# Output projection of a hybrid decoder layer: seven block products in place of eight, activations of projection and feed-forward in paired tiles, the second norm split in wide pieces

## The chip, the cores and the metric

The kernel runs on one core of a Trainium2 chip. The metric is the device time of one execution in microseconds (us). A core has a matrix engine (TensorE, PE in the profile, with its weight loads as PEld), a vector engine (VectorE, DVE), a scalar engine (ScalarE, ACT), a general engine (GpSimd, POOL) and a queue engine that issues transfers (SyncE, SP). Each works through its own list of instructions in order; they wait for each other through semaphores.

## The reference: one decoder layer

512 positions, width 1024, everything in float32. What matters here:

```python
h = rmsnorm(x, norm1_w)
proj = h @ w_in                       # q, k, v of 6 + 6 attention heads, and GLA's inputs
y_a = dilated_attention(...)          # 6 heads of 64
y_b = gla(...)                        # 4 heads of 64, gated linear attention
y_c = moba_attention(...)             # 6 heads of 64
mix = concat([y_a, y_b, y_c])         # 512 x 1024
x = x + mix @ w_out                   # the output projection, 1024 x 1024
h2 = rmsnorm(x, norm2_w)
x = x + square(relu(h2 @ w_ff1)) @ w_ff2     # 1024 -> 4096 -> 1024
out = rmsnorm(x, final_norm_w)
```

## The kernel before

**Products in three parts.** TensorE multiplies in fp32r, a shorter format than float32. So every operand is split in two: a high part, cast on ScalarE (`wh` of a weight, `mh`, `yh`, `Ah` of an activation), and the low rest, a subtraction on VectorE (`wl`, `ml`, `yl`, `Al`). A product is then three matmuls: high by high, high by low, low by high. A weight piece is 128x1024; it comes by a DMA on SP's queue into a raw tile (`wraw`, `w2raw`), and its split takes one cast and one subtraction.

**The stages.** `main` (line 1364) is the list of TensorE's dense work: the first projection of GLA's inputs (`av`, `bq`, `bk` in the profile), the values and gates (`vps`), q and k of six pairs of heads (`qkps`), the values of the second group (`vps`), the output projection `out_proj` (line 1009, `ops`), and the feed-forward network `ffn` (line 1277). Attention is filled in between: scores (`sps`), transposes of the softmax (`ptp`), and the product with the values (`po`) in `values` (line 784), once for each two pairs of heads. GLA ends with two transposes (`yp`). Each result for the mix goes through `mix_out` (line 514), which makes `mh` and `ml` straight from PSUM, for one of eight blocks of 128 columns of the mix.

**The output projection** makes four tiles of 128 positions (t) by two halves of 512 columns. Each tile and half is a sum over the 8 blocks of the mix, three matmuls of 128x512 each. It begins with the blocks that are there first (the order is in `KO`), for t = 0 and 1, and does the last two blocks, from the last heads, after `po` of these heads. When a tile's half is done, `x2_out` (line 981) adds it to the residual `x3` (VectorE) and takes the sum of squares (ScalarE, `junk`); after the second half `inv_rms` (line 969) makes the factor `y` in four tiny steps that go between ScalarE and VectorE. `y_out` (line 991) scales the tile (`y0`, shown as `y`), turns it with eight transposes of 128x128 (`yps`), and splits the result in pieces of 128x128, with the norm's weight: 4 casts and 4 subtractions for each half.

**The feed-forward network** goes in four quarters of 1024 hidden columns. `f` is the first product; ScalarE applies relu into a tile `h` of 128x512 and a square follows. The second product is done in blocks by a scheme of Strassen's kind: `h` of a quarter and the quarter of `w_ff2` are each cut into 2x2 blocks, `a_parts` (line 1072) makes sums and differences of the activation blocks (`s`), `sums2` (line 340) those of the weight blocks, and seven products of blocks (`products`, line 372; `f2X` to `f2W`) replace eight. The results are added to `x3` by `add` (line 1150). A block of the activations is two tiles of 128x2x256; since `h` is 128x512 with both halves of the positions in one row, `a_parts` reads a block in pieces of 128x256. The first four columns of `f` are made in two halves of 256 positions, since only the first tiles are normalised by then.

**What sets the order.** Every stage is a generator that gives out instructions; `Plan` (line 98) takes the instruction that could start first by its own table of costs (ties by priority), and the list of each engine is written in that order. Nothing is reordered on the chip. Buffers are tokens: 23 large ones of 128x1024 (`big`), pairs of split weights (`w`), pairs of split activations (`part`), and the PSUM banks. All instructions are recorded at line 128 of the file, so in the profile they are told apart by their tiles.

Of the kernel before, what the change touches and what calls it, by code (L numbers as in the profile page):

```python
# [30 lines left out]
NH = 4  # L31


class Op:


    def __init__(self, eng, method, args, kw):
# [9 lines left out]
        self.outs = [o.tensor.name for o in outs]  # L47
        self.ins = [a.tensor.name for a in inner]
# [148 lines left out]
def hybrid_block_kernel(ctx: ExitStack, tc: tile.TileContext, x0_d, xT_d, x_d, w0_d, wv_d, wqk_d, wo_d, w1_d, w2_d,  # L197
                        ba_d, wa2_d, gw_d, fw_d, rb_d, oh_d, cst_d, lm_d, out_d):
# [15 lines left out]
    def big(name, dt=F32, shape=(128, 1024)):  # L214
        return wp.tile(list(shape), dt, name=name, tag="big", bufs=BIGS)

# [34 lines left out]
    nwh = consts.tile([128, KT], F32)  # L251
# [11 lines left out]
    xh = [slot("xh", F32R) for _ in range(KT)]  # L263
    xl = [slot("xl", F32R) for _ in range(KT)]
# [10 lines left out]
    def fetch():  # L275
        for key, src, n in pieces[1:]:
# [36 lines left out]
    def cut():  # L313
        for key, src, n in pieces:
# [6 lines left out]
            if key[0] == "1" and (key[1] % 8 == 0 and key[1] or key[1] == 31):  # L321
                yield from cut2((key[1] - 1) // 8)
# [5 lines left out]
    def fetch2():  # L328
        yield ("wait", ("raw", ("1", 5)))
        for c in range(NC):  # L330
# [7 lines left out]
            spawn(sums2(c), 4)  # L338

# [32 lines left out]
    def products(c):  # L372


        if c < NC - 1:
# [5 lines left out]
    def cut2(c):  # L381
        for o, (n, *_) in enumerate(products(c)):
# [9 lines left out]
            for _ in range(2):  # L392
                if n > 2:
                    give("big")
                    give("raw2")
# [55 lines left out]
    def row_scale():  # L451
# [16 lines left out]
        yield DVE.tensor_scalar(nwh, nw[:, 1], -0.5, None, op0=OP.mult)  # L468
# [43 lines left out]
    mh, ml = [None] * 8, [None] * 8  # L512
# [38 lines left out]
    def gla():  # L551
# [117 lines left out]
        yield ("wait", "G")  # L669
        for i in range(2):  # L670
# [9 lines left out]
            yield DVE.tensor_tensor(oB[i], oB[i], G[i], op=OP.mult)  # L680
        for f in range(2):
            r = "gm"[f] * (1 + f)
# [4 lines left out]
            spawn(mix_out(3 + f, yp, r), 1)  # L687
# [48 lines left out]
    def attention(e):  # L736
# [3 lines left out]
        for p in range(6):  # L740
# [14 lines left out]
            if ("sps", p) in plan.done:  # L755
# [3 lines left out]
                if p == 4:  # L759
                    give("w")  # L760
                    give("w")
                if p == 5:
                    for _ in range(3):
                        give("big")
                    give("w")
                    fire("scores")
# [17 lines left out]
    def values():  # L784


        for ps_ in ((0, 1), (2, 3), (4, 5)):
# [24 lines left out]
            for p, po, r in zip(ps_, pos, "og"):  # L812
                spawn(mix_out(p if p < 3 else p + 2, po, r), 1)
# [29 lines left out]
    def v_out(g, t, acc):  # L843
# [12 lines left out]
        yield DVE.tensor_scalar(sg, rg, 80.0, None, op0=OP.min)  # L856
        yield DVE.tensor_tensor(rg, rg, gw, op=OP.mult)
# [80 lines left out]
    def gate(i):  # L938


        sg, rg = gates[i]
# [4 lines left out]
        yield DVE.scalar_tensor_tensor(d, sg, 1.0, y, op0=OP.add, op1=OP.mult)  # L946
        yield DVE.scalar_tensor_tensor(d, d, -2.0, y, op0=OP.add, op1=OP.mult)
        yield DVE.tensor_tensor(rg, d, rg, op=OP.mult)
# [6 lines left out]
    yh, yl = [slot("yh", F32R) for _ in range(KT)], [slot("yl", F32R) for _ in range(KT)]  # L955
# [25 lines left out]
    def x2_out(t, half, acc, r):  # L981
        yield DVE.tensor_tensor(x3[t, half], acc, x3[t, half], op=OP.add)
        give(r)
        yield from square_sum(t, half)
        if half:
# [4 lines left out]

    def y_out(t, half, y):
        y0 = slot("y0")
        yield Any(DVE.tensor_scalar(y0, x3[t, half], y, None, op0=OP.mult), ACT.activation(y0, x3[t, half], AF.Copy, scale=y))
        r = ("pt", "pt") if t != 1 else ("o", "g")
        r = r[half]
# [3 lines left out]
        ts = slice(t * 128, (t + 1) * 128)  # L999
        ks = range(half * 4, half * 4 + 4)  # L1000
        src = [pt[:, i * 128:(i + 1) * 128] for i in range(4)]
        for i, k in enumerate(ks):
            yield ACT.activation(yh[k][:, ts], src[i], AF.Copy, scale=nwh[:, k:k + 1])
        for i, k in enumerate(ks):
            yield DVE.scalar_tensor_tensor(yl[k][:, ts], src[i], nwh[:, k:k + 1], f32(yh[k][:, ts]), op0=OP.mult, op1=OP.subtract)
            fire(("y", t, k))
        give(r)

    def out_proj():

        w = {}
        accs = {}

        def step(t, i, halves=(0, 1)):
            k = KO[i]
            if i not in w:
                yield ("wait", ("w", ("o", i)))
                w[i] = loaded.pop(("o", i))
            yield ("wait", ("mix", k))
            wh, wl = w[i]  # L1020
            ts = slice(t * 128, (t + 1) * 128)
            for half in halves:
                fs = slice(half * 512, half * 512 + 512)
                yield [PE.matmul(accs[t][half], xx[k][:, ts], ww[:, fs], start=(i + j == 0), stop=(i == 7 and j == 2))
                       for j, (xx, ww) in enumerate(((mh, wh), (ml, wh), (mh, wl)))]

        def take(t):
            r = "mm" if t % 2 == 0 else "s"
            accs[t] = []
# [499 lines left out]
```

## Time and profile before

| | |
|---|---|
| median of 3 runs | 585.29 us (585.05 to 585.51) |
| the profiled execution | 586.21 us, span from first to last instruction 584.4 us |
| TensorE busy | 575.6 us, 98% of the span |
| VectorE busy | 420.8 us, 72% |
| ScalarE busy | 325.4 us, 56% |
| DMA | 62.00 MB, mean 106 GB/s |
| granted TensorE clock, mean | 0.997 |

Busy time is the time in which an engine has an instruction in work. TensorE's instructions overlap (the next begins before the one before has left the array), so the mean duration of a matmul is longer than the step from one to the next, and the step is read from a row of the chain: its time over its count. The chain of waits, followed back from the last instruction, tells which engine sets the time at each moment. In the order listings below, as in the profile, `out<-in` names the tiles, and `x4` is a row that stands four times.

### The profile page before, as it was taken

The numbers are of one execution on the slowest core, as the hardware profiler recorded it, in microseconds if no ns is written. First come the engines' busy times: TensorE is split into PE (matmuls) and PEld (weight loads), VectorE is DVE, ScalarE is ACT, GpSimd is POOL, SyncE is SP. The second block draws the span as 40 slices with busy tenths as digits, with TensorE's granted clock in tenths as the row PEclk, the third lists the DMA queues.
The fourth block names the chain that finished last, engine by engine and source line by source line (L and its number), as shares of the span: only waits on it lengthen the run. The fifth ranks groups of instructions, "written<-read, shape, count | busy, mean of one in ns | idle before, by whom it ended". The sixth has DMA issues, their size and how long they took to land.

```text
span 584.4 us, 8148 instructions
## 1 busy us (share of the span) xinstructions
PE 575.6 (98%) x3030; PEld 478.9 (82%) x3030; DVE 420.8 (72%) x812; ACT 325.4 (56%) x611; POOL 19.0 (3%) x36
## 2 busy tenths in 40 slices
PE   9999999999999999999999999999999999999995
PEld 8988888977888588899888888888888888888884
DVE  6879999987774405566479954599925699755896
ACT  6756476887787305546457334575244664354654
POOL 7000000000000000000000000000000000000021
PEclk9999999999999999999999999999999999999998
DMA  9920334322342600194004732025621046201003
GB/s 313 341 74 2 109 89 147 91 73 85 119 123 73 252 1 0 59 372 127 20 1 153 243 109 72 1 72 183 213 73 37 1 138 223 72 1 36 1 0 146
DMA packets 20696, 62.00 MB, mean 106 GB/s; under 512 B 2482, under 2 KB 3168, under 8 KB 20656
## 3 DMA queue, kind: packets, MB, share of 16 engines
q1 hardware_dynamic: 19728, 59.84, 31.3%
q0 software_dynamic: 640, 1.10, 0.6%
q8 instruction: 24, 0.39, 0.3%
q10 hardware_dynamic: 288, 0.53, 0.3%
q14 instruction: 16, 0.13, 0.1%
HBM read 59.34 MB, written 2.13 MB: 105 GB/s over the span
## 4 chain that ended last, share of the span: by engine, by line
PE 97%; DVE 1%; ACT 0%; issue 0%; DVEq 0%
PE f L128 30%; PE f2X L128 14%; PE qkps L128 11%; PE vps L128 8%; PE ops L128 7%; PE f2Z L128 6%; PE f2Y L128 4%; PE sps L128 3%; PE po L128 2%; PE ptp L128 2%; PE av L128 2%; PE f2W L128 2%; PE lp L128 1%; PE bk L128 1%; PE bq L128 1%; PE op L128 1%
## 5 line engine op out<-in xcount | busy, mean ns | idle before, releaser
L128 DVE TENSOR_TENSOR wl<-wraw,wh 128x1024 fp32r<-128x1024 f32 (+1 forms) x68 | 78.3, 1160 | 39.6 <-ACT wh L128 33.9
L128 PE MATMUL f<-yh,wh 128*128 128x512 f32 (+1 forms) x288 | 105.3, 366 | 0.0
L128 PE MATMUL f<-yl,wh 128*128 128x512 f32 (+1 forms) x288 | 105.3, 365 | 0.0
L128 PE MATMUL f<-yh,wl 128*128 128x512 f32 (+1 forms) x288 | 105.2, 365 | 0.0
L128 ACT ACTIVATE wh<-wraw 128x1024 fp32r<-128x1024 f32 (+1 forms) x67 | 67.2, 1013 | 58.4 <-PE f L128 23.2
L128 DVE TENSOR_TENSOR wl<-w2raw,wh 128x1024 fp32r<-128x1024 f32 x48 | 59.4, 1243 | 48.5 <-ACT wh L128 44.7
L128 ACT ACTIVATE wh<-w2raw 128x1024 fp32r<-128x1024 f32 x48 | 50.3, 1054 | 49.2 <-PE f L128 39.7
L128 PEld LDWEIGHTS f<-yl,wh 128*128 128x128 f32 x288 | 54.3, 189 | 8.8
L128 PEld LDWEIGHTS f<-yh,wh 128*128 128x128 f32 x288 | 54.3, 189 | 8.7
L128 PEld LDWEIGHTS f<-yh,wl 128*128 128x128 f32 x288 | 54.3, 189 | 8.7
L128 PE MATMUL f2X<-wl,Ah 128*128 128x512 f32 (+1 forms) x128 | 49.4, 386 | 0.0
L128 PE MATMUL f2X<-wh,Al 128*128 128x512 f32 (+1 forms) x128 | 49.4, 386 | 0.0
L128 PE MATMUL f2X<-wh,Ah 128*128 128x512 f32 (+1 forms) x128 | 49.4, 386 | 0.0
L128 PE MATMUL qkps<-xh,wh 128*128 128x512 f32 x96 | 39.3, 409 | 1.0 <-DVE tk L128 1.0
L128 PE MATMUL qkps<-xh,wl 128*128 128x512 f32 x96 | 37.6, 391 | 0.0
L128 PE MATMUL qkps<-xl,wh 128*128 128x512 f32 x96 | 37.5, 390 | 0.0
L128 ACT ACTIVATE P<-P,mn 128x512 f32<-128x512 f32 (+3 forms) x48 | 26.5, 553 | 14.1 <-DVE mn L128 14.0
L128 ACT ACTIVATE h<-f 128x512 f32<-128x512 f32 x32 | 18.6, 582 | 18.7 <-PE f L128 18.7
L128 DVE CUSTOM_DVE_ANT_0 P<-sps,nb 128x512 f32<-128x512 f32 (+3 forms) x48 | 22.4, 483 | 8.5 <-PE sps L128 7.9
L128 ACT ACTIVATE junk<-x 128x512 f32<-128x512 f32 (+1 forms) x16 | 9.8, 615 | 32.8 <-DVE x L128 32.8
L128 PEld LDWEIGHTS f2X<-wh,Al 128*128 128x128 f32 x128 | 24.1, 188 | 4.9
L128 PEld LDWEIGHTS f2X<-wh,Ah 128*128 128x128 f32 x128 | 24.0, 188 | 4.9
(248 smaller groups left out, 1187.8 us busy)
## 6 DMA issues: line engine op xcount, KB each, us to landing
wraw<-in_w SPq DMA_DIRECT2D x32, 512.0 KB, 3.6
w2raw<-in_w SPq DMA_DIRECT2D x32, 512.0 KB, 4.3
wraw<-in_wqk SPq DMA_DIRECT2D x12, 512.0 KB, 4.0
wraw<-in_wv SPq DMA_DIRECT2D x8, 512.0 KB, 6.4
wraw<-in_wo SPq DMA_DIRECT2D x8, 512.0 KB, 3.6
nb<-tab SPq DMA_DIRECT2D x12, 256.0 KB, 4.0
x<-in_x SPq DMA_DIRECT2D x8, 256.0 KB, 4.8
wraw<-in_w SPq DMA_DIRECT2D x7, 264.0 KB, 5.2
```

What stands on the lines that cost most here:

```text
L128: getattr(getattr(self.nc, op.eng), op.method)(*op.args, **op.kw)
```

## The change

The output projection becomes chunk 0 of the same block scheme that the second product of the feed-forward network uses, which has chunks 1 to 4 now. `w_out` is handed in with its rows in the order of `KO` and joined to `w_ff2`. The mix is written to PSUM-sized halves of large tiles (`halves`, `mix_out`), as plain float32, so that `a_parts(0)` can form and split block sums; `fetch0` loads `w_out` in eight pieces (`woraw`), `sums0` makes the block sums of the weights, `cut2(0)` splits them, and `ff2(0)` runs the seven products in the order 0, 4, 6, 2, 3, 1, 5. `products` gives for each the accumulator (X, W or Y) and the block (half of the positions, half of the columns) to which it adds. The positions' second half (t = 2, 3) is complete first, so the first columns of `f` begin with it.

`h` is now a tile of 128x2x2x256, shared by two columns of `f`, in which the two tiles of one block lie together; `a_parts` works on 128x512 where it worked on 128x256. `y_out` multiplies by the norm's weight before the transposes (a row of weights, `nw2`, broadcast to 128 partitions, is loaded for it), and splits each half by one cast and one subtraction of 128x512. There are 27 large buffers in place of 23 and 34 of 128x512 in place of 52; the 16 split tiles of x lie in four tiles of 128x4x512 (`quarters`), which the 16 of y take over. The product G of GLA's gate waits later in its generator, and the transposes `yp` use other PSUM banks.

```diff
-KO = (3, 4, 0, 1, 2, 5, 6, 7)
+KO = (0, 1, 3, 4, 2, 5, 6, 7)
-BIGS, SLOTS, WPAIRS = 23, 52, 5
-NC = 4
+BIGS, SLOTS, WPAIRS, SCRATCH = 27, 34, 5, 4096
+NC = 5
...
             if key[0] == "x3":
+                yield ("wait", ("values", 4 if key[2] else 2))
                 x3[key[1:]] = slot("x3")
...
+            if key == ("v", 1, 3):
+                yield from cut2(0)
...
+    def fetch0():
+        yield ("wait", ("qk", 5))
+        spawn(sums0(), 3)
+        for q in ((0, 0), (1, 1), (0, 1), (1, 0)):
+            quads[q] = []
+            for ip in range(2):
+                yield ("take", "big")
+                quads[q].append(big("woraw"))
+                yield SP.dma_start(quads[q][ip], w2_d[0, q[0], q[1], ip])
+            fire(("quad", 0, q))
...
+    def sums0():
+        yield ("wait", ("quad", 0, (0, 0)))
+        t, b6 = [None] * 2, [None] * 2
+        b11 = quads[0, 0]
+        B[0] = {0: b11, 4: t, 2: t, 6: b6}
...
+            yield DVE.tensor_tensor(t[ip], b22[ip], b12[ip], op=OP.subtract)
...
+            yield DVE.tensor_tensor(b12[ip], b12[ip], b11[ip], op=OP.subtract)
...
+            yield DVE.tensor_tensor(t[ip], t[ip], b11[ip], op=OP.add)
...
+            yield DVE.tensor_tensor(b6[ip], b21[ip], t[ip], op=OP.subtract)
...
     def products(c):
+        if not c:
+            return ((0, "X", True, ((0, 0),)), (4, "W", True, ((1, 1),)), (6, "W", False, ((1, 0),)), (2, "X", False, ((1, 0),)),
+                    (3, "X", False, ((1, 1),)), (1, "Y", True, ((0, 0),)), (5, "X", False, ((0, 1),)))
...
-    def mix_out(k, src, res=None):
-        mh[k] = slot("mh", F32R)
-        ml[k] = slot("ml", F32R)
-        yield ACT.activation(mh[k], src, AF.Copy)
-        yield DVE.tensor_tensor(ml[k], src, f32(mh[k]), op=OP.subtract)
-        if res:
-            give(res)
-        fire(("mix", k))
+    def halves(c, f):
+        j, ip, i = f // 4, f // 2 % 2, f % 2
+        if (j, ip) not in hs[c]:
+            yield ("take", "big")
+            hs[c][j, ip] = big("h", F32, (128, 2, 2, 256))
+        return hs[c][j, ip][:, :, i]
+    def mix_out(k, src, res):
+        f = KO.index(k)
+        h = yield from halves(0, f)
+        yield ACT.activation(h, split2(src), AF.Copy)
+        give(res)
+        fire(("h", 0, f))
...
-            r = "gm"[f] * (1 + f)
+            r = "go"[f]
             yield ("take", r)
             yp = bank(r, "yp")
...
     def y_out(t, half, y):
         y0 = slot("y0")
-        yield Any(DVE.tensor_scalar(y0, x3[t, half], y, None, op0=OP.mult), ACT.activation(y0, x3[t, half], AF.Copy, scale=y))
+        yield ("wait", "nw2")
+        yield DVE.scalar_tensor_tensor(y0, x3[t, half], y, st["nw2"][:, half * 512:half * 512 + 512], op0=OP.mult, op1=OP.mult)
...
         yield [PE.transpose(pt[:, i * 128:(i + 1) * 128], y0[:, i * 128:(i + 1) * 128], ident) for i in range(4)]
-        for i, k in enumerate(ks):
-            yield ACT.activation(yh[k][:, ts], src[i], AF.Copy, scale=nwh[:, k:k + 1])
-        for i, k in enumerate(ks):
-            yield DVE.scalar_tensor_tensor(yl[k][:, ts], src[i], nwh[:, k:k + 1], f32(yh[k][:, ts]), op0=OP.mult, op1=OP.subtract)
+        yield ACT.activation(hi, src, AF.Copy)
+        yield DVE.tensor_tensor(lo, src, f32(hi), op=OP.subtract)
...
     def a_parts(c):
-                    yield ACT.activation(hi[:, i], src[i], AF.Copy)
-                    yield DVE.tensor_tensor(lo[:, i], src[i], f32(hi[:, i]), op=OP.subtract)
+                yield ACT.activation(hi, src[ip], AF.Copy)
+                yield DVE.tensor_tensor(lo, src[ip], f32(hi), op=OP.subtract)
...
         def ff1_first():
-            rs = ("mm", "mm", "o", "g")
+            rs = ("s", "s", "mm", "mm")
             for f in range(NH):
...
-                yield from half_dense(f, slice(0, 256), range(2))
+                yield from half_dense(f, slice(256, 512), range(2, 4))
             for f in range(NH):
-                yield from half_dense(f, slice(256, 512), range(2, 4))
+                yield from half_dense(f, slice(0, 256), range(2))
...
     def main():
         yield from v_proj(1)
-        yield from out_proj()
+        yield from ff2(0)
         yield from ffn()
```

TensorE's list has 2616 rows in place of 2640. How the change moves instructions, at three places. The first is TensorE's list around the transposes of the first normalised tile, before:

```order
L128 MATMUL ops<-wh,mh 128x512
L128 MATMUL ops<-wh,ml 128x512
L128 MATMUL ops<-wl,mh 128x512
L128 MATMUL yps<-cst,y_2632 128x128 x4
L128 MATMUL yps<-cst,y_2633 128x128 x4
L128 MATMUL ops<-wh,mh 128x512
```

and now, for t = 2 (`f2Y` is product 1, `f2X` behind it product 5, the last):

```order
L137 MATMUL f2Y<-wl,Ah 128x512
L137 MATMUL yps<-cst,y_2758 128x128 x4
L137 MATMUL yps<-cst,y_2759 128x128 x4
L137 MATMUL f2Y<-wh,Ah 128x512
L137 MATMUL f2Y<-wh,Al 128x512
L137 MATMUL f2Y<-wl,Ah 128x512
L137 MATMUL f2X<-wh,Ah 128x512
```

Before, the first transposes stand 87 `ops` matmuls ahead of the first `f`; now they stand 27 matmuls ahead of it, the four of t = 3's first half 12 matmuls, and those of t = 0 and 1 behind the first 18 `f` matmuls.

The second is VectorE's list at the norm of the last tiles, before (`x` is a tile of `x3`, `m`, `tmp`, `y` at 128x1 the tiny steps of the norm):

```order
L128 SCALAR_TENSOR_TENSOR yl<-yps,nwh,yh 128x128 x8
L128 TENSOR_TENSOR x_2428<-ops,x_2428 128x512
L128 TENSOR_TENSOR wl<-wraw,wh 128x1024
L128 TENSOR_SCALAR m<-ssq 128x1
L128 TENSOR_TENSOR wl<-wraw,wh 128x1024 x2
L128 TENSOR_TENSOR x_2430<-ops,x_2430 128x512
```

and now, from the add of product 3 to the scaling of t = 2 (`s` is a sum of activation blocks):

```order
L137 TENSOR_TENSOR x_2491<-f2X,x_2491 128x512
L137 TENSOR_TENSOR Al<-s_2668,Ah 128x512
L137 TENSOR_TENSOR wl<-wraw,wh 128x1024
L137 SCALAR_TENSOR_TENSOR m<-ssq,m 128x1
L137 TENSOR_TENSOR x_2493<-f2X,x_2493 128x512
L137 TENSOR_TENSOR Al<-s_2679,Ah 128x512
L137 SCALAR_TENSOR_TENSOR tmp<-y,m 128x1
L137 TENSOR_TENSOR wl<-wraw,wh 128x1024
L137 SCALAR_TENSOR_TENSOR y<-tmp,y 128x1
L137 TENSOR_TENSOR x_2425<-f2Y,x_2425 128x512
L137 SCALAR_TENSOR_TENSOR m<-ssq,m 128x1
L137 SCALAR_TENSOR_TENSOR y_2758<-x_2444,y,nw_2472 128x512
```

Splits of activations and of the next weights, adds and the norm's steps share the list now. From the first split of block A22 (product 6) to the last `yl` of t = 3 VectorE's list has 62 instructions: 12 subtractions `wl` of 128x1024, 10 `Al`, 6 sums `s`, 13 adds to `x`, 4 scalings `y`, 4 `yl`, all of 512 columns, and 13 tiny ones.

The third is SP's list of transfers ahead of the projection, before (`nb` is a bias table of the attention, `wraw<-in_w` behind the `x` rows the first weights of the feed-forward network):

```order
L128 DMA wraw<-in_wo 128x1024 x4
L128 DMA x_2413<-in_x 128x512
L128 DMA x_2415<-in_x 128x512
L128 DMA x_2417<-in_x 128x512
L128 DMA x_2419<-in_x 128x512
L128 DMA x_2424<-in_x 128x512
L128 DMA x_2426<-in_x 128x512
L128 DMA x_2428<-in_x 128x512
L128 DMA x_2430<-in_x 128x512
L128 DMA wraw<-in_w 128x1024 x7
```

and now:

```order
L137 DMA nb<-tab 128x512 x4
L137 DMA woraw<-in_w 128x1024 x8
L137 DMA x_2425<-in_x 128x512
L137 DMA x_2438<-in_x 128x512
L137 DMA x_2444<-in_x 128x512
L137 DMA x_2446<-in_x 128x512
L137 DMA nw_2472<-in_nw 128x1024
L137 DMA x_2475<-in_x 128x512
L137 DMA x_2489<-in_x 128x512
L137 DMA x_2491<-in_x 128x512
L137 DMA x_2493<-in_x 128x512
L137 DMA wraw<-in_w 128x1024 x6
```

All eight pieces of `w_out` are loaded behind the last `nb`; the first four `x` tiles wait for the second group of `po`, and the norm's weights and the other four for the third.

More of the change, by code (lines that the diff above doesn't have):

```diff
@@ L392, in cut2 @@
             for _ in range(2):
-                if n > 2:
+                if not c and n not in (0, 4):
+                    give("big")
+                if c and n > 2:
                     give("big")
@@ L979, in inv_rms, with x2_out @@
         st["inv", t] = y
-    def x2_out(t, half, acc, r):
-        yield DVE.tensor_tensor(x3[t, half], acc, x3[t, half], op=OP.add)
-        give(r)
+    def x2_out(t, half):
+        both = t in ssq
         yield from square_sum(t, half)
-        if half:
+        if both:
             yield from inv_rms(t)
@@ L1065, in h_out, with a_parts @@
-    def h_out(c, f, acc, h, r="mm"):
-        h[f] = slot("h")
-        yield ACT.activation(h[f], acc, AF.Relu)
-        give(r)
-        yield Any(ACT.activation(h[f], h[f], AF.Square), DVE.tensor_tensor(h[f], h[f], h[f], op=OP.mult), late=dict(vector=1.0))
+        yield Any(ACT.activation(h, h, AF.Square), DVE.tensor_tensor(h, h, h, op=OP.mult), late=dict(vector=1.0))
         fire(("h", c, f))
-    def a_parts(c, h):
-        one, two = slice(0, 256), slice(256, 512)
+    def a_parts(c):
+        ends = c in (0, NC - 1)
@@ L1076, in new @@
         def new(name, dt=F32):
             return slot(name, dt, (128, 2, 256))
-        def split(n, ip, src):
-            yield ("take", "part")
-            hi, lo = new("Ah", F32R), new("Al", F32R)
-            if isinstance(src, list):
-                for i in range(2):
-                    yield ACT.activation(hi[:, i], src[i], AF.Copy)
-                    yield DVE.tensor_tensor(lo[:, i], src[i], f32(hi[:, i]), op=OP.subtract)
-            else:
-                yield ACT.activation(hi, src, AF.Copy)
-                yield DVE.tensor_tensor(lo, src, f32(hi), op=OP.subtract)
-            A[c, n, ip] = (hi, lo)
-            fire(("A", c, n, ip))
@@ L1092, in quad, with split @@
-        def quad(j, cols, ip):
-            return [h[4 * j + 2 * ip + i][:, cols] for i in range(2)]
-        s1, s2, s3, s4 = {}, {}, {}, {}
+        def split(n, src):
+            for ip in range(2):
+                yield ("take", "part")
+                hi, lo = new("Ah", F32R), new("Al", F32R)
+                yield ACT.activation(hi, src[ip], AF.Copy)
+                yield DVE.tensor_tensor(lo, src[ip], f32(hi), op=OP.subtract)
+                A[c, n, ip] = (hi, lo)
+                fire(("A", c, n, ip))
@@ L1097, in urgent, with quad, made @@
+        def quad(j, half):
+            return [hs[c][j, ip][:, half] for ip in range(2)]
+        def made(name, a, b, op):
+            d = []
+            for ip in range(2):
+                d.append(new(name))
+                yield DVE.tensor_tensor(d[ip], a[ip], b[ip], op=op)
+            return d
         def urgent(o):
@@ L1099, in urgent, with give_h @@
                 yield ("prio", 1.4 + o)
+        def give_h():
+            give("big")
+            give("big")
+        if not c:
+            yield ("wait", ("v", 1, 0))
+            yield ("prio", 1)
         for f in range(4):
             yield ("wait", ("h", c, f))
-        for ip in range(2):
-            yield from split(0, ip, quad(0, one, ip))
-        for ip in range(2):
-            s3[ip] = new("s3")
-            for i in range(2):
-                yield DVE.tensor_tensor(s3[ip][:, i], quad(0, one, ip)[i], quad(0, two, ip)[i], op=OP.subtract)
+        q00, q01 = quad(0, 0), quad(0, 1)
+        yield from split(0, q00)
+        if not c:
+            yield ("wait", ("values", 2))
+            yield ("prio", 0.5)
+        s3 = yield from made("s3", q00, q01, OP.subtract)
         yield from urgent(1)
-        if c == NC - 1:
-            for ip in range(2):
-                yield from split(4, ip, s3[ip])
+        if ends:
+            yield from split(4, s3)
         yield from urgent(2)
@@ L1343, in ff2 @@
                     if i == 1 and q == 1 and js[-1] == len(cut_[q]) - 1:
-                        give_w()
+                        if not c and n == 5:
+                            give("big")
+                            give("big")
+                        else:
+                            give_w()
                         give("part")
```

279 lines of the change are left out of this document (139 added, 140 removed).

## The prediction

> **What bounds the kernel now.** I read the page first: the share of each engine, then the chain of waits.
>
> ```profile
> span 584.4 us, 8148 instructions
> PE 575.6 (98%) x3030; PEld 478.9 (82%) x3030; DVE 420.8 (72%) x812; ACT 325.4 (56%) x611; POOL 19.0 (3%) x36
> PE 97%; DVE 1%; ACT 0%; issue 0%; DVEq 0%
> ```
>
> TensorE is busy for 98% of the span and holds 97% of the chain. So a matmul that goes away is worth its whole step, and work that moves to another engine is free as long as TensorE does not wait for it. The list of what TensorE waited for, with engine PE alone, is complete in three rows (total, times, longest):
>
> ```profile
> PE warm L128 <- DVE eps L128: 1.1, 1, 1.1
> PE qkps L128 <- DVE tk L128: 1.0, 1, 1.0
> PE yps L128 <- DVE y L128: 0.2, 1, 0.2
> ```
>
> After its start TensorE waits 1.2 us in all. The windows by stage (length, then busy time of PE, PEld, DVE, ACT, POOL; last but two the granted clock) show what cover the other engines have:
>
> ```profile
> 165.00:193.00 28.00, 28.00 (x141) 23.06 (x140) 16.91 (x42) 19.21 (x41) 0.00 (x0) 1.00 0.34 106
> 193.00:205.00 12.00, 12.00 (x78) 6.19 (x76) 3.30 (x4) 3.56 (x6) 0.00 (x0) 1.00 0.63 238
> 205.00:249.00 44.00, 43.82 (x207) 36.23 (x206) 18.65 (x53) 17.00 (x50) 0.00 (x0) 1.00 0.08 25
> 575.00:585.00 10.00, 2.80 (x24) 2.60 (x22) 5.52 (x18) 3.64 (x12) 0.00 (x0) 0.78 0.57 210
> ```
>
> The output projection is 193 to 249. VectorE has 22 of 56 us of work there: it is the stage with the most room, and the one that gets the new work.
>
> **What is removed.** The groups by form give the matmuls of the projection, and the chain in order of time their step:
>
> ```profile
> L128 PE MATMUL ops<-wh,mh 128*128 128x512 f32 x64 | 25.4, 397 | 0.0
> L128 PE MATMUL ops<-wl,mh 128*128 128x512 f32 x64 | 24.9, 390 | 0.0
> L128 PE MATMUL ops<-wh,ml 128*128 128x512 f32 x64 | 24.9, 389 | 0.0
> ...
> 192.87 0.68 PE ops L128 x3
> ...
> 200.27 4.46 PE po L128 x32
> 204.73 21.31 PE ops L128 x93
> 229.86 1.06 PE yps L128 x8
> 240.50 0.87 PE yps L128 x8
> 248.87 5.75 PE f L128 x48
> 300.21 5.44 PE f2X L128 x24
> ```
>
> 192 matmuls become 168: seven products of 24. The 24 that go are one block product, and the same shape in the feed-forward network takes 5.44 us for 24 (0.227 us a step; the means of 390 ns overlap). The `ops` row gives 21.31 / 93 = 0.229, the same. TensorE's list falls from 2640 to 2616 rows, so nothing else is added there. **Term 1: -5.4 us.** The transposes `yps` remain 32, in more and shorter groups; the two rows of eight differ by 0.2 us, and I put 0.1 us to three more changes between the kinds. **Term 2: +0.1 us.**
>
> **The wait at 133 us.** This is the piece of the chain that holds the 1.0 us wait:
>
> ```profile
> 131.74 0.50 ACT mh L128
> 132.26 0.53 DVE ml L128
> 132.87 0.69 DVE tk L128
> 133.60 5.05 PE qkps L128 x21
> ```
>
> The split of GLA's part of the mix (`mh`, `ml`) stands ahead of `tk` on VectorE, and its bank is one of the two that `qkps` uses. Now `yp` uses other banks and there is no `ml` there, which takes out 0.53 us or the whole wait. But the interleaving of attention is rearranged from 85 to 190 us, and could bring a wait like it elsewhere. Bounds -1.0 and +1.0; I take -0.5, the length of `ml`. **Term 3: -0.5 us.**
>
> **What VectorE gets.** Its durations, from the order in time and the groups by form:
>
> ```profile
> 189.14 3.50 DVE L128 TENSOR_TENSOR wl<-wraw,wh 128x1024 fp32r<-128x1024 f32 x3 [5.27 <-ACT wh L128]
> 194.58 1.23 DVE L128 TENSOR_TENSOR wl<-wraw,wh 128x1024 fp32r<-128x1024 f32 x1 [1.94 <-ACT wh L128]
> 222.79 0.16 DVE L128 SCALAR_TENSOR_TENSOR m<-ssq,m 128x1 f32<-128x1 f32 x1 [0.53 <-ACT junk L128]
> 223.46 0.22 DVE L128 SCALAR_TENSOR_TENSOR tmp<-y,m 128x1 f32<-128x1 f32 x1 [0.51 <-ACT y L128]
> 224.20 0.15 DVE L128 SCALAR_TENSOR_TENSOR y<-tmp,y 128x1 f32<-128x1 f32 x1
> 224.26 0.68 DVE L128 TENSOR_TENSOR x<-ops,x 128x512 f32<-128x512 f32 x1
> 224.87 0.48 DVE L128 TENSOR_SCALAR y<-x,y 128x512 f32<-128x512 f32 x1
> 226.30 0.16 DVE L128 SCALAR_TENSOR_TENSOR m<-ssq,m 128x1 f32<-128x1 f32 x1 [0.89 <-ACT junk L128]
> 227.88 0.87 DVE L128 SCALAR_TENSOR_TENSOR yl<-yps,nwh,yh 128x128 fp32r<-128x128 f32 x3 [1.42 <-ACT yh L128]
> ...
> L128 DVE SCALAR_TENSOR_TENSOR xl<-xT,nw,xh 128x512 fp32r<-128x512 f32 x7 | 5.1, 746 | 0.0
> ```
>
> A step of 128x1024 is (3.50 - 1.23) / 2 = 1.14 us; one of 128x512 is 224.87 - 224.26 = 0.61. The new scaling `y0` with three inputs is nearest to `xl`, 0.06 us longer than an add: 0.67. A tiny one is 0.06 (224.20 to 224.26) to 0.14 (223.46 to the next add): 0.1.
>
> Ahead of the last `po` (165 to 205 us) VectorE now has 7 `wl` and 8 sums of 128x1024, 4 `Al`, 2 sums and 1 add of 512: 15 x 1.14 + 7 x 0.61 = 21.4 us, in place of 5 `wl` and 4 `ml`, 8.1 us. With the 16.91 + 3.30 us that lie there it is 33.5 of 40 us. This fits under the value projection, `po` and the first 9 matmuls; uncovered it would cost up to its 13.3 us. ScalarE's added casts (two weight pieces more than before and four `Ah`) find 17 us of room in the same windows. I cost both at nothing.
>
> **The hand-over to the feed-forward network** is where a wait comes in. Time zero is the first matmul of the projection (192.9 before). Everything behind product 4 needs block sums with the last two heads, so VectorE's row of 62 instructions from the first `Al` of A22 cannot begin before both `po` are over: 9 x 0.227 + 2 x 4.46 = 11.0, then two copies and a cast on ScalarE at about 0.6 each:
>
> ```profile
> L128 ACT ACTIVATE mh<-po 128x512 fp32r<-128x512 f32 x4 | 2.4, 598 | 8.4 <-PE po L128 8.4
> L128 ACT ACTIVATE Ah<-s 128x512 fp32r<-128x512 f32 x32 | 19.4, 619 | 13.4 <-DVE s L128 13.4
> ```
>
> so at 12.8. The row is 12 `wl` x 1.14 + 33 of 512 (`Al`, `s`, add, `yl`) x 0.61 + 4 `y0` x 0.67 + 13 x 0.1 = 13.7 + 20.1 + 2.7 + 1.3 = 37.8 us. Laid end to end it ends with the last `yl` of t = 3 at 50.6. TensorE without a wait has done its 168 steps, two `po`, and the `yps` of t = 2 and 3 at 38.1 + 8.9 + 2 x 0.87 = 48.7; 12 half-wide `f` (5.75 / 48 = 0.12 each) bring it to 50.2, where the fifth row of `yh` needs just this `yl`. So VectorE, with 18.65 of 44 us of work before, is full, and even with no gap TensorE waits 0.4 us. Gaps there will be: the norm's chain goes from add to `junk` to `m` to `y` on two engines. One tile's chain before left VectorE idle for 0.53 + 0.51 + 0.89 + 1.42 = 3.4 us (the brackets above), and the two tiles now run one behind the other with weight splits between. Bounds: 0.4 (all filled) and 3.8 (one tile's gaps open). I take 2.4, a little over the middle, since the adds also wait for their products. It comes at the `yps` of t = 2 and t = 3 and at the fifth row of `f`. **Term 4: +2.4 us, less the 0.2 us of the old `yps` wait.** The `yps` of t = 0 and 1 have (96 - 18) x 0.12 = 9.4 us of `f` between them and their use.
>
> On the clock: it is granted 1.00 in every window above but the last, after TensorE's final matmuls (0.78). The Trainium skill ("TensorE: Matmul & The Clock Gate", "Why this matters for your kernels") says that an idle gap above some 3 us lowers the clock to half. The falling clock at the end agrees. With the wait in three pieces around matmuls the sum is unchanged; were it one gap, the estimate by that page is another 1.7 us (half of the 3.4 us window that its section "What's actually happening" gives).
>
> **The wide pieces in the network.** VectorE saves per quarter, but TensorE's list shows no wait in the network at all, so I cost the saving at nothing; if the sums came late, the rows of the hand-over show the price of each. The last quarter's steps behind the last matmul are unchanged. The first weights of `f` are issued behind the last `x` tiles now, after both `po`, at about 205 instead of 191 (the row of SP's queue below), and are used from 192.9 + 48.7 = 241.6 on.
>
> ```profile
> wraw<-in_wo SPq DMA_DIRECT2D x8, 512.0 KB, 3.6
> x<-in_x SPq DMA_DIRECT2D x8, 256.0 KB, 4.8
> ...
> 191.15 5.01 SPq L128 DMA_DIRECT2D wraw<-in_w  x4
> ```
>
> At 3.6 us each, they have the time.
>
> **Sum.** -5.4 + 0.1 - 0.5 + 2.4 - 0.2 = -3.6 us. The profiled execution took 586.2 us with a span of 584.4; the median of the runs is 585.29. Span 584.4 - 3.6 = 580.8, and by the same difference for the median 585.3 - 3.6 = **581.7 us**, 0.6% faster. The likeliest case's own range, by the bounds of terms 3 and 4: 585.3 - 5.4 + 0.1 - 0.2 - 1.0 + 0.4 = 579.2 to 585.3 - 5.4 + 0.1 - 0.2 + 1.0 + 3.8 = 584.6; both ends together are unlikely, so 580.0 to 583.9.
>
> **Rivals.**
>
> *The whole gain.* VectorE's gaps are filled, and the wait at 133 us is gone: 579.2. For it speaks that the transposes before stood where TensorE waited only 0.2 us for all four tiles; against it, that VectorE then had 25 us of slack, and has none now.
>
> *The last tiles of x come late.* The second four `x` tiles are issued behind the norm's weights, and only after `po`, at 11.0. The add of product 4 needs the third of them at 11.0 + 15 x 0.227 + half of 5.44 = 17.1, and everything of product 2 is queued behind it on VectorE. By the DMA rows the weights land after 3.6, and tiles after another 4.8 at most: 19.4, a gap of 2.3 us in a full list, which the hand-over pays: 581.7 + 2.3 = 584.0, within or just below 0.2%. Against it: in the first windows the loads overlapped, and one or two us after the norm's weights would do.
>
> *VectorE and TensorE in turns: slower.* The adds wait for a product's end, and the next product's splits stand behind them in the same list. The first splits lead TensorE by 5.9 us (`Al` of A22 is ready at 14.0, product 6 begins at 11.0 + 15 x 0.227 + 5.44 = 19.9). If late sums or weight pieces eat this lead, each of the five later products shows its splits: an add, a weight split and an `Al`, 0.61 + 1.14 + 0.61 = 2.4 us each less what overlaps, say 1.5, so 7.5 us: 581.7 + 7.5 = 589.2. It decides from a VectorE delay of 5.9 us on at product 6. For it: the list is full. Against it: per product VectorE has 37.8 / 7 = 5.4 us of work to TensorE's 5.44, so a lead once gained is kept.
>
> That the change does not do what it says is excluded by the 24 missing rows.
>
> **Chances.** Forecast 0.57, whole gain 0.18, late tiles 0.13, in turns 0.12. A measurement of this kernel tells about 0.2% (1.2 us) from no change. Faster than 584.1: 0.55 of the first, 0.18, and 0.04 of the third: 0.77. The same: 0.02 + 0.08 + 0.01 = 0.11. Slower: 0.01 + 0.11 = 0.12. The range leaves out most of the last case and a little below the second: 578.9 to 585.2.
>
> **What the new profile would show.** Term 1: 168 `f2` matmuls where 192 `ops` stood, at 0.227 us a step. Term 3: no `qkps` wait above 0.5 us. Term 4: PE waits of 0.5 to 1.5 us each for `y` before `yps` and for `yl` before `f`, and VectorE over 90% busy from 205 to 245. Wrong if PE waits inside the products (for `Al` or `wl`), if the network shows waits, or if PE waits under 1 or over 4 us in the hand-over.

## The result

| | before | changed |
|---|---|---|
| median of the runs side by side | 585.40 us (4 runs, 585.05 to 586.04) | 579.84 us (4 runs, 578.93 to 580.04) |
| profiled execution, span | 586.21, 584.4 | 580.01, 577.9 |

The ratio is 0.9901, with a 95% interval of 0.9884 to 0.9918: 1.0% faster, 5.6 us. A second comparison (the control below) gave 0.9897 (0.9883 to 0.9910). Forecast were 581.7 us and a gain of 3.6. The ratios here and below are those on record; they differ from the quotients of the medians by up to 0.0013, so no effect under 1 us is read from a ratio alone. One of the six executions of the experiment e5 with the order held was a slow one of 1480.97 us, and its time below is the median of the other five.

The page of the changed kernel, its shares and the chain by engine:

```profile
span 577.9 us, 8055 instructions
PE 569.4 (99%) x3006; PEld 474.8 (82%) x3006; DVE 444.5 (77%) x774; ACT 329.3 (57%) x575; POOL 18.7 (3%) x36
PE 96%; DMA 2%; DVE 1%; issue 0%; ACT 0%; DVEq 0%
```

TensorE's busy time fell by 6.2 us, the span by 6.5. That is more than the 5.6 us between the medians: the profiled execution of the kernel before lies 0.8 us above its median and that of the changed kernel 0.2 us above its own, and 0.3 us more passes outside the span now (580.01 - 577.9 against 586.21 - 584.4). VectorE has 24 us more work in the whole. What TensorE waited for:

```profile
PE warm L137 <- DVE eps L137: 1.1, 1, 1.1
PE vps L137 <- ACT rg L137: 0.6, 1, 0.6
PE f L137 <- DVE yl L137: 0.2, 1, 0.2
```

The two old waits (1.0 for `tk`, 0.2 before `yps`) are gone, and two new ones stand there, 0.8 us together. None is inside a block product.

Where the 6.5 us come from is read from the chain in order of time, by the start of the first row of four stages. Before (the rows of the projection, 192.87, and of the first block product of the network, 300.21, stand in the prediction):

```profile
30.68 2.73 PE vps L128 x12
59.35 0.68 PE qkps L128 x3
```

and now:

```profile
30.53 2.74 PE vps L137 x12
59.89 3.40 PE qkps L137 x15
191.88 0.68 PE f2X L137 x3
293.71 5.44 PE f2X L137 x24
```

| stretch (from the first matmul of one stage to that of the next) | before | changed | difference |
|---|---|---|---|
| up to the first `vps` | 30.68 | 30.53 | -0.15 |
| first `vps` to first `qkps` | 28.67 | 29.36 | +0.69 |
| first `qkps` to the projection | 133.52 | 131.99 | -1.53 |
| projection and hand-over, to the first block product of the network | 107.34 | 101.83 | -5.51 |
| from there to the end | 284.2 | 284.2 | 0.0 |

The projection stretch is 101.82 or 101.83 us in all five profiles of kernels that leave it as it is (the changed kernel, its control, e3, e7 and e10). The last stretch differs by 0.3 us over all thirteen profiles, and the first by 1.1 us, so the -0.15 in the first row means nothing. Whole runs scatter by 1 us. So the experiments are judged by these stretches beside the times.

The hand-over, where a wait of 2.4 us was forecast, in windows of the changed kernel:

```profile
204.00:246.00 42.00, 41.78 (x211) 35.22 (x210) 41.32 (x71) 27.99 (x53) 0.00 (x0) 1.00 0.55 189
```

VectorE is busy for 41.32 of 42 us, 98%, and TensorE for 41.78. Both are full at once. The order of time on VectorE shows the first and the last row of the list that the prediction laid end to end, and some of the norm's steps:

```profile
204.59 1.28 DVE L137 TENSOR_TENSOR Al<-h,Ah 128x512 fp32r<-128x512 f32 x2
...
229.14 0.69 DVE L137 TENSOR_TENSOR Al<-s,Ah 128x512 fp32r<-128x512 f32 x1
229.74 0.22 DVE L137 SCALAR_TENSOR_TENSOR tmp<-y,m 128x1 f32<-128x1 f32 x1
229.87 1.22 DVE L137 TENSOR_TENSOR wl<-wraw,wh 128x1024 fp32r<-128x1024 f32 x1
231.00 0.16 DVE L137 SCALAR_TENSOR_TENSOR y<-tmp,y 128x1 f32<-128x1 f32 x1
231.19 0.69 DVE L137 TENSOR_TENSOR x<-f2Y,x 128x512 f32<-128x512 f32 x1
...
242.19 0.69 DVE L137 TENSOR_TENSOR yl<-yps,yh 128x512 fp32r<-128x512 f32 x1
```

None of these rows has an idle time in brackets: while `tmp` waits for ScalarE an `Al` runs, and between `tmp` and `y` a weight split. From 204.59 to 242.19 + 0.60 the list took 38.2 us, and its laid-out sum was 37.8.

One line of the page misleads: the chain has 2% of DMA, 8.7 us of `w2raw` from 232 on. These pieces are read by VectorE only at 249.41, behind all of this. In an experiment with the same hand-over (e3, narrow pieces in the network, below) the chain goes through VectorE's steps at that place.

### The profile page after: what moved, and what is told of

Read it like the earlier page. It is cut to its first block, busy times and chain, and to the rows that moved or that the text cites. A ratio compares the mean times of both kernels' runs of the same rounds, so it can differ in the third digit from the quotient of the medians.

```text
span 577.9 us, 8055 instructions
## 1 busy us (share of the span) xinstructions
PE 569.4 (99%) x3006; PEld 474.8 (82%) x3006; DVE 444.5 (77%) x774; ACT 329.3 (57%) x575; POOL 18.7 (3%) x36
## 4 chain that ended last, share of the span: by engine, by line
PE 96%; DMA 2%; DVE 1%; issue 0%; ACT 0%; DVEq 0%
PE f L137 30%; PE f2X L137 17%; PE qkps L137 11%; PE vps L137 8%; PE f2Z L137 6%; PE f2Y L137 4%; PE f2W L137 4%; PE sps L137 3%; PE ptp L137 2%; PE po L137 2%; PE av L137 2%; DMA w2raw<-in_w 2%; PE lp L137 1%; PE bk L137 1%; PE bq L137 1%; PE op L137 1%
## 5 line engine op out<-in xcount | busy, mean ns | idle before, releaser
L137 DVE TENSOR_TENSOR wl<-wraw,wh 128x1024 fp32r<-128x1024 f32 (+1 forms) x60 | 68.4, 1152 | 24.5 <-ACT wh L137 24.3
L137 ACT ACTIVATE wh<-wraw 128x1024 fp32r<-128x1024 f32 (+1 forms) x59 | 58.0, 1002 | 30.4 <-PE f2X L137 18.6
L137 PE MATMUL f2X<-wh,Ah 128*128 128x512 f32 (+1 forms) x160 | 62.3, 390 | 0.0
L137 PE MATMUL f2X<-wl,Ah 128*128 128x512 f32 (+1 forms) x160 | 61.9, 387 | 0.0
L137 PE MATMUL f2X<-wh,Al 128*128 128x512 f32 (+1 forms) x160 | 61.9, 387 | 0.0
L137 PEld LDWEIGHTS f2X<-wh,Ah 128*128 128x128 f32 x160 | 30.1, 188 | 7.6 <-issue 1.6
L137 PEld LDWEIGHTS f2X<-wl,Ah 128*128 128x128 f32 x160 | 30.1, 188 | 6.2
L137 PEld LDWEIGHTS f2X<-wh,Al 128*128 128x128 f32 x160 | 30.1, 188 | 6.0
L137 DVE TENSOR_TENSOR x<-f2X,x 128x512 f32<-128x512 f32 (+1 forms) x41 | 26.8, 674 | 6.5 <-PE f2X L137 6.3
```

The source lines that it names most:

```text
L137: getattr(getattr(self.nc, op.eng), op.method)(*op.args, **op.kw)
```

## Experiments

Each kernel was compared with the kernel before on the same chip. "Projection stretch" is the fourth row of the table above: 107.34 before, 101.83 now.

**The 24 matmuls alone** (e1). The kernel before, without one block of the mix:

```diff
             yield ("wait", ("mix", k))
+            if i == 5:
+                return
             wh, wl = w[i]
```

> The kernel before, with one of the eight blocks of the mix left out of the output projection: its 24 matmuls are not made, its weights are still loaded and split. The result lacks that block. Theory 'steps': the gain of the change is the time of 24 matmul steps on a TensorE that never waits, so -5.4 us (580.0), PE waits as before (1.0 and 0.2). Rival 'arrangement': a part of the 5.6 us comes from the new order around the projection, and 24 matmuls alone bring 4.5 us or less.

580.85 us against 585.72; ratio 0.9907 (0.9890 to 0.9923); span 579.0. The projection stretch is 101.90, 5.44 us less than before, which is the price of one block product to the hundredth. The waits stayed:

```profile
PE qkps L128 <- DVE tk L128: 1.0, 1, 1.0
PE yps L128 <- DVE y L128: 0.2, 1, 0.2
```

So 'steps' holds: the changed kernel's 5.51 in this stretch is these 24 steps and nothing else of size (in e1 the planner also moved a few transposes and adds of the stretch). All that the block scheme adds on VectorE and ScalarE is hidden, but for the 0.2 us before `f`, which stand where 0.2 us before `yps` stood.

**The banks of GLA's transposes** (e4). The kernel before with

```diff
-            r = "gm"[f] * (1 + f)
+            r = "go"[f]
```

> The kernel before, with GLA's two transposes in the banks that the change gives them (o for m), all else as before. Theory 'bank': the wait of qkps for tk (1.0 us) came from the bank that the transposes and their split held, so it goes, and the span falls by 0.5 to 1.0 us (584.4 to 584.9). Rival 'order': the wait went because GLA's end was moved in the list, and it stays here within 0.3 us.

584.53 us against 585.72; ratio 0.9983 (0.9975 to 0.9992). The wait for `tk` is gone from the list:

```profile
PE warm L128 <- DVE eps L128: 1.1, 1, 1.1
PE av L128 <- ACT wh L128: 0.2, 1, 0.2
PE yps L128 <- DVE y L128: 0.2, 1, 0.2
```

The stretch from `qkps` to the projection fell from 133.52 to 132.28, by 1.24 of the 1.53 us that it falls in the change. The profiled span hardly moved (584.3), since in that execution the clock was lowered at 50 us, which made the stretch before it 1.4 us longer; of this below. 'Bank' holds. It holds together with the order of the neighbouring rows, which the planner made anew: some thirty of TensorE's rows (scores, transposes and products of q and k) changed place, and no run separates the two. The split `ml` is still there in this kernel, so it was not `ml` that made the wait.

**Narrow pieces in the network** (e3). In the changed kernel:

```diff
-                yield ACT.activation(hi, src[ip], AF.Copy)
-                yield DVE.tensor_tensor(lo, src[ip], f32(hi), op=OP.subtract)
+                for i in range(2) if c and n in (0, 1, 6) else (slice(0, 2),):
+                    yield ACT.activation(hi[:, i], src[ip][:, i], AF.Copy)
+                    yield DVE.tensor_tensor(lo[:, i], src[ip][:, i], f32(hi[:, i]), op=OP.subtract)
...
-                yield DVE.tensor_tensor(d[ip], a[ip], b[ip], op=op)
+                for i in range(2) if c else (slice(0, 2),):
+                    yield DVE.tensor_tensor(d[ip][:, i], a[ip][:, i], b[ip][:, i], op=op)
```

> The changed kernel with the feed-forward network's activation sums and splits in pieces of 128x256 again (chunks 1 to 4; the tiles stay paired). VectorE gets some 1.5 us more in each chunk. Theory 'covered': TensorE never waits in the network, so no change within 0.2% (579.8), no PE wait in the network. Rival 'needed': VectorE is busy for 36 of 38 us in the second products and falls behind, 1 us or more per chunk, 583 to 586.

579.94 us; ratio 0.9898 (0.9884 to 0.9911), the changed kernel's own. The window of one second product, in the narrow kernel:

```profile
375.00:413.00 38.00, 38.00 (x169) 31.50 (x168) 36.35 (x52) 22.34 (x29) 0.00 (x0) 1.00 0.54 171
```

and in the changed one:

```profile
375.00:413.00 38.00, 38.00 (x170) 31.47 (x168) 35.72 (x44) 21.80 (x27) 0.00 (x0) 1.00 0.57 172
```

The paired tiles save VectorE 0.6 us of busy time in 38 us, and TensorE is at 38.00 of 38.00 either way. 'Covered' holds: in the network they bring nothing.

**The gate's steps** (e7, and once more, e10, beside the changed kernel itself, e9). The groups of VectorE steps that the change hands out as one are handed out one by one:

```diff
-        yield [DVE.tensor_scalar(sg, rg, 80.0, None, op0=OP.min), DVE.tensor_tensor(rg, rg, gw, op=OP.mult)]
+        yield DVE.tensor_scalar(sg, rg, 80.0, None, op0=OP.min)
+        yield DVE.tensor_tensor(rg, rg, gw, op=OP.mult)
...
-        yield [DVE.scalar_tensor_tensor(d, sg, 1.0, y, op0=OP.add, op1=OP.mult),
-               DVE.scalar_tensor_tensor(d, d, -2.0, y, op0=OP.add, op1=OP.mult),
-               DVE.tensor_tensor(rg, d, rg, op=OP.mult)]
+        yield DVE.scalar_tensor_tensor(d, sg, 1.0, y, op0=OP.add, op1=OP.mult)
+        yield DVE.scalar_tensor_tensor(d, d, -2.0, y, op0=OP.add, op1=OP.mult)
+        yield DVE.tensor_tensor(rg, d, rg, op=OP.mult)
```

> The changed kernel with the steps of GLA's gate on VectorE given out one by one as before, not in groups. Theory 'gate': the new wait of vps for ACT rg (0.6 us at 51 us) comes from the grouped steps, which let the gate's exponentials start ahead of the value's copy on ScalarE; it goes, -0.3 to -0.6 us, if the new order brings no other. Rival: the wait stays or another takes its place, no change within 0.3 us.

579.62 us, ratio 0.9892 (0.9878 to 0.9905), span 577.5. TensorE's list of waits has no `rg`:

```profile
PE warm L137 <- DVE eps L137: 1.1, 1, 1.1
PE f L137 <- DVE yl L137: 0.2, 1, 0.2
```

and `vps` to `qkps` takes 28.64 instead of 29.36, as before the change. This is the place in the changed kernel, on TensorE and on ScalarE:

```profile
50.62 0.40 PE L137 MATMUL vps<-wl,xh 128*128 128x512 f32 x1
50.85 0.49 PE L137 MATMUL ktp<-cst,ek 128*128 128x128 f32 x3
51.95 0.51 PE L137 MATMUL vps<-wh,xh 128*128 128x512 f32 x1 [0.60 <-ACT rg L137]
51.05 0.47 ACT L137 ACTIVATE v<-vps,rstd 128x256 f32<-128x256 f32 x1 [0.75 <-PE vps L137]
51.43 0.47 ACT L137 ACTIVATE rg<-vps,nrstd 128x256 f32<-128x256 f32 x1
51.78 0.49 ACT L137 ACTIVATE kend<-ktp 128x384 f32<-128x384 f32 x1
```

The expectation blamed the gate's exponentials, which now stand ahead of the copy on ScalarE. But they do not delay it: ScalarE sat idle for 0.75 us before `v`, waiting for TensorE. What the groups changed is the order on both engines: the transposes `ktp` now stand behind the tile's last `vps` (50.62), where they stood three `vps` ahead of it, and their copy `kend` stands behind `rg`. So one of the two banks is held by the tile until `rg` is done, the other by `ktp` until `kend` is done, and the next tile's `vps` (51.95) waits for the first. In the kernel before, `kend` began at 50.89, ahead of `v`, and the next tile began without a wait. The second time:

> The changed kernel itself, for comparison on the same chip. All theories: 0.990 of the kernel before.

> The changed kernel with the gate's steps given out one by one, a second time and beside the changed kernel itself. Theory 'gate': 0.6 to 0.7 us below the changed kernel, all of it between the first value matmul and the first q or k matmul (28.6 in place of 29.4 us). Rival: no difference that holds.

e9 gave 579.60 us (0.9897, 0.9883 to 0.9910), e10 579.36 us (0.9894, 0.9879 to 0.9909); the stretch was 28.60 in e10. In the trace the 0.7 us are there both times (0.16 of them are lost again in the next stretch, 132.15 against 131.99), and it is the gate's grouping, by the order that came of it, that made the new wait. In the times the two kernels can't be told apart. So this version beats the kernel before, by 1.1%, and is ahead of the changed one by the trace alone.

**Has VectorE slack in the hand-over?** Two experiments add work to its list with the order of all lists held (the planner is told that the added steps cost nothing, or what the wide ones cost). Four additions of 128x512 (e5, held):

```diff
+            if not c and n == 6:
+                extra = slot("extra")
+                for _ in range(2):
+                    yield DVE.tensor_tensor(extra, x3[t, half], x3[t, half], op=OP.add)
```

> The changed kernel with four more VectorE operations of 128x512 (an addition into a tile nobody reads), two behind each add of product 6, 4 x 0.61 = 2.4 us in all; the lists of all engines are otherwise word for word those of the changed kernel. Theory 'full': VectorE's list from the split of A22 to the last yl has no slack, so TensorE waits 2.0 to 2.6 us more, 582.0 to 582.4. Rival 'slack': the list is only filled up, its parts are early where they are needed, and TensorE waits under 0.8 us more.

582.34 us; ratio 0.9929 (0.9914 to 0.9945); span 580.1. The projection stretch is 104.30, 2.47 us longer: the added work, 4 x 0.61, one for one. TensorE's waits (its rows bear L139, as this kernel's file has two lines more):

```profile
PE f2X L139 <- DVE x L139: 1.0, 1, 1.0
PE yps L139 <- DVE y L139: 0.7, 1, 0.7
PE vps L139 <- ACT rg L139: 0.6, 1, 0.6
PE f L139 <- DVE yl L139: 0.2, 1, 0.2
```

The first two rows are new; one of them is inside a block product. They are the time in which TensorE had nothing in work: from one matmul's begin to the next one's it lost 1.17 and 0.86 us there, and the rest of the 2.47 lies in the steps behind. 'Full' holds to the tenth. But the same four steps, known to the planner (e5, order made anew):

> The same four operations, but known to the planner, so that the order is made anew: some weight splits of the network's first columns move behind the norm. Theory 'full': the work that moves was not due yet, so part of the 2.4 us is taken up; 0.5 to 1.5 us. Rival 'critical': all 2.4 us show, as with the held order.

580.06 us; ratio 0.9884 (0.9867 to 0.9901); stretch 101.70, nothing lost, and no wait in the hand-over:

```profile
PE warm L137 <- DVE eps L137: 1.1, 1, 1.1
PE vps L137 <- ACT rg L137: 0.6, 1, 0.6
```

Both theories of this run missed it, on the low side. VectorE's list is full, but partly with work that is not due: the weight splits of the network's first columns. Five of these stood ahead of the last `yl` of t = 3; the planner moved two of them (2.3 us) behind it, and 2.4 us of new work found room.

**The norm in narrow pieces** (e2), order held:

```diff
-        yield ACT.activation(hi, src, AF.Copy)
-        yield DVE.tensor_tensor(lo, src, f32(hi), op=OP.subtract)
+        for i in range(4):
+            op = ACT.activation(hi[:, i], src[:, i], AF.Copy)
+            op.cost = 0.517 / 4
+            yield op
+        for i in range(4):
+            op = DVE.tensor_tensor(lo[:, i], src[:, i], f32(hi[:, i]), op=OP.subtract)
+            op.cost = 0.607 / 4
+            yield op
```

> The changed kernel with the norm's split in pieces of 128x128 again (4 casts and 4 subtractions for a half in place of one each), the lists otherwise the same. A step of 128x128 was 0.26 us on both engines in the kernel before, so a half costs 1.1 in place of 0.6 us on each. Theory 'full': the four halves of t = 2 and 3 lengthen VectorE's list by 2.0 us, and ScalarE's pieces ahead of them add to it: +2.0 to +3.0 us. Rival 'slack': under 0.8 us.

580.96 us; ratio 0.9905 (0.9889 to 0.9922); stretch 102.84, 1.0 us longer. The effect has the sign of 'full', but half the size. The price was wrong; two rows of VectorE's steps in this kernel's chain:

```profile
242.56 0.79 DVE yl L137 x4
245.86 1.59 DVE yl L137 x8
```

Four pieces take 0.79 to 0.80 us, not 1.1: the step is 0.20. The pieces of the kernel before, at 0.26, were another operation, with the norm's weight as a third input. Against 0.60 for the wide one it is 0.2 us a half, 0.8 for the four halves, and 1.0 was measured with ScalarE's pieces. So the wide pieces of the norm are worth 1.0 us with this order.

**Work taken from VectorE** (e6): the first five `wl` of the network left out, 5.7 us, with the order made anew.

```diff
+        if key[0] == "1" and key[1] < 5:
+            yield ACT.activation(lo[:, :1], src[:, :1], AF.Copy)
+            loaded[key] = (hi, hi)
```

> The changed kernel without the five subtractions wl of the network's first five weight pieces (5.7 us of VectorE; the third matmul of these columns reads wh in place of wl, so the result lacks these low parts). Theory 'balanced': TensorE waits only 0.2 us in the hand-over, so taking VectorE work away brings 0.2 us at most. Rival 'VectorE sets the stage': 1 us or more.

580.11 us; ratio 0.9894 (0.9877 to 0.9910); stretch 101.73, 0.1 us less. The wait for `yl` is gone, and no more than that was there to gain: 'balanced' holds.

**24 matmuls put back** (e8), lists held:

```diff
+                        if not c and n == 3 and m < 3:
+                            more = [PE.matmul(bk[b_, q][h_][:, :cs.stop - cs.start], aa[:, i, ts], ww[:, ws], start=False,
+                                              stop=False, skip_group_check=True) for aa, ww in ((ah, wh), (al, wh), (ah, wl), (ah, wh))]
```

> The changed kernel with 24 matmuls more in product 3 (they add the high parts' products once more into its accumulators, so the result is off there), all lists otherwise as they are; that is as many matmuls as eight products would have. Theory 'both full': TensorE's list costs step for step, +5.44 us, less the 0.2 us for which it waits in the hand-over, since VectorE gets 5.4 us of room: +5.2 us from the first matmul of the projection to the first block product of the network (101.84 to 107.1 us). Rival 'VectorE sets the stage': the room is used, and 24 matmuls cost 3 us or less.

585.41 us; ratio 0.9989 (0.9981 to 0.9998); stretch 107.26, 5.43 us longer. TensorE's steps count in full here too, and VectorE got room:

```profile
204.00:246.00 42.00, 42.00 (x195) 34.84 (x194) 36.14 (x59) 25.17 (x46) 0.00 (x0) 1.00 0.52 178
```

36.14 of 42 us in place of 41.32. The 0.2 us for `yl` stayed, against the expectation. The room lies ahead of two adds of product 3, which wait for its longer sum:

```profile
227.97 0.69 DVE L137 TENSOR_TENSOR x<-f2X,x 128x512 f32<-128x512 f32 x1 [2.25 <-PE f2X L137]
233.41 0.69 DVE L137 TENSOR_TENSOR x<-f2X,x 128x512 f32<-128x512 f32 x1 [2.94 <-PE f2X L137]
```

From the second of these adds to the last `yl` of t = 3 VectorE's list is as full as before, and as long: 13.7 us (233.41 to 247.13; 228.54 to 242.19 in the changed kernel). So what leaves the 0.2 us is this last part of the list, which begins with the add of product 3, and room ahead of it does not help.

## Why the prediction was right, and where it failed

**The number owes something to luck.** 579.84 us lies in the range of 578.9 to 585.2, and the kernel got faster, as was forecast. But the case that was given 0.57, with a wait of 2.4 us in the hand-over and 580.0 to 583.9 us, did not happen; the range holds the measured time since it was drawn wide enough for the rival that was given 0.18. By the prediction's own sign (TensorE waits under 1 us in the hand-over) its fourth term is wrong.

**Term 1, the 24 matmuls: right in cause and size.** -5.4 was said, 5.44 measured alone (e1), 5.43 the other way (e8), and the whole projection stretch moved by 5.51. The bound was read rightly: on a TensorE without waits a matmul is worth its step.

**Term 2** (0.1 us for more changes between transposes and matmuls) doesn't show: 5.51 instead of 5.44 leaves nothing for it.

**Term 3, the wait at 133 us: right in its cause, mis-sized.** The bank was the cause (e4, with the order that goes with it). -0.5 was taken, the length of `ml`, which the wait did not hang on; the stretch gained 1.53, of which the banks alone brought 1.24 (e4). The other 0.29 no run took apart. The other half of the step, that the new order could bring a wait like it elsewhere, came true too, at 51 us, in a part before the window that was named: 0.69 us for the gate's grouped steps (e7). The prediction did not follow that part of the diff to the two banks that `vps` and `ktp` share. Together it is -0.84 where -0.5 was said.

**Term 4, the hand-over: the step that failed.** "Bounds: 0.4 (all filled) and 3.8 (one tile's gaps open). I take 2.4, a little over the middle, since the adds also wait for their products." Measured is 0.2, a little below even the lower bound, and at the place that the laid-out sum named, the fifth row of `f`. This sum was good: begin 12.7 us after the projection's first matmul (12.8 said), 38.2 us long (37.8 said). What was wrong is the term for the gaps. It was taken from a stage in which VectorE had 18.65 us of work in 44; an idle time in a stage with slack is no price for a full one. (The four brackets are not one tile's either: the 0.89 before `m` at 226.30 belongs to the next tile. A single tile of that stage has about the same, 0.79 + 0.50 + 1.94 = 3.2 us from 238 to 242.) Here every gap had another row in it, an `Al`, an add or a weight split. That an order with such rows can hide the gaps was in the order listing, since the tiny steps stand apart with other work between, and the prediction saw it ("with weight splits between") and priced half the gaps all the same.

**The wide pieces.** Free in the network, as said (e3). In the norm they were part of the laid-out sum only, and are worth 1.0 us in it (e2).

**The rivals.** The whole gain (579.2) is what happened in its mechanism, VectorE's gaps filled and the wait at 133 us gone, and the time is 0.6 us off, with the new wait at 51 us against it. "The last tiles of x come late" fell on its premise: the row of SP's queue shows the transfers issued before both `po` were over (198.59 + 4.46 = 203.05).

```profile
196.29 0.33 SPq L137 DMA_DIRECT2D nw<-in_nw  x1
196.71 1.81 SPq L137 DMA_DIRECT2D x<-in_x  x4
```

The wait that the diff writes is the planner's, which sets the place in the list; on the chip SP waits only for the buffer. They were issued 5 to 7 us ahead of what the prediction allowed (11.0 us after the projection's first matmul, at 202.9), and the add of product 4 waited for its product, not for the tile. "In turns" needed a delay of 5.9 us and there was none. The clock stayed at 1.00 in the hand-over, where TensorE was idle for 0.2 us in all; what a long gap does there was not put to the test.

## What to carry to other kernels

On an engine without waits, price removed work by its step, and ask of the added work only whether it fits under that engine when it is laid end to end on its own; idle times copied from a stage with slack overstate what a full list leaves open. A full helper engine is not yet a limit: see how much of its list is not due, since that moves when the order is made anew (2.4 us more cost 2.5 us with the order held, and nothing without). In a diff that touches an order, follow every regrouped step to the bank or buffer that it frees later, however small it looks.

## What the runs showed of the hardware

The clock of TensorE fell to half in the middle of work, with TensorE busy all the time ahead of it in the profile. In three of the thirteen profiled executions, of three kernels (e4, e6 and the control), it dropped for 3.4 us, from between 48.9 and 49.9 us on; this is the control, in windows:

```profile
44.00:46.50 2.50, 2.50 (x40) 1.95 (x42) 2.50 (x7) 0.72 (x2) 0.00 (x0) 1.00 0.00 0
46.50:48.00 1.50, 1.50 (x45) 1.43 (x41) 1.47 (x6) 1.29 (x3) 0.00 (x0) 1.00 0.00 0
48.00:49.00 1.00, 1.00 (x8) 0.95 (x8) 1.00 (x4) 0.97 (x3) 0.00 (x0) 0.93 0.00 0
49.00:50.00 1.00, 1.00 (x4) 0.71 (x4) 1.00 (x4) 0.39 (x2) 0.00 (x0) 0.50 0.00 0
50.00:51.00 1.00, 1.00 (x4) 0.70 (x3) 1.00 (x4) 0.00 (x0) 0.00 (x0) 0.50 0.00 0
```

and the matmuls ahead of it and in it, in order of time:

```profile
45.75 1.85 PE L137 MATMUL lp<-kq 32*128 32x64 f32 x60
47.53 1.05 PE L137 MATMUL dps<-cst,qk 128*128 128x4 f32 x8
48.44 0.49 PE L137 MATMUL vps<-wh,xh 128*128 128x512 f32 x1
...
49.53 0.63 PE L137 MATMUL vps<-wh,xh 128*128 128x512 f32 x1
49.96 0.63 PE L137 MATMUL vps<-wh,xl 128*128 128x512 f32 x1
```

What stands ahead is 64 matmuls of GLA that use 32 rows and 64 columns (60 of them in the window shown), and 8 of four columns, 2.9 us in all: busy in the profile, but with little of the array in use. In each of the three, the 3.4 us ahead of the fall hold all of them (45.59 to 48.44 in the control, where the clock fell at 48.9). The same 64 alone, 1.9 us at about 55 us and again at about 63 us, stand in all the traces, and the clock fell behind them in none. The Trainium skill ("TensorE: Matmul & The Clock Gate", "What's actually happening") has the clock fall after an idle window of about 3.4 us, in windows that run freely. The length agrees, 3.4 us each time. That no idle engine is needed differs from it, and here the measurement decides; that the small matmuls count as idle, and that the phase of the window decides in which execution it happens, fits these three and is still a guess, since no run here tested it. It costs 1.0 to 1.4 us when it happens (`vps` to `qkps` 30.39 in the control and 29.36 in the changed kernel; 30.09 in e4 and 28.67 before), and so may be a part of the scatter of 1 us between runs.
